# SSM layer of a two-layer hybrid: state updates as four unsplit products on strips of 32 rows, and another split of the PSUM banks

## The chip, the cores and the metric

The kernel runs on one core of a Trainium2 chip. The metric is the device time of one execution, in microseconds. Before the change it is 1091.27 us, the median of three runs (1090.25 to 1092.51).

## The reference, cut to what matters

One inference step of a two-layer encoder for 256 prompt tokens (one sequence) and 128 sample tokens (8 sequences of 16), 384 rows in all, D_MODEL 1024. Layer 0 mixes with short convolutions and attention, layer 1 with a state-space scan (SSM); each layer ends in a convolutional feed-forward network. The change lies in layer 1's mixer:

```python
def odd_mixer(h, conv_state, ssm_state, w_in, conv_w, conv_b, dt_bias, a_log, d_skip, norm_w, w_out):
    proj = h @ w_in
    z, xbc, dt_raw = jnp.split(proj, [D_INNER, D_INNER + CONV_DIM], axis=-1)   # 2048, 3072, 32
    xbc, new_conv = causal_dwconv(xbc, conv_state, conv_w, conv_b)
    xbc = jax.nn.silu(xbc)
    xs, bm, cm = jnp.split(xbc, [D_INNER, D_INNER + SSM_GROUPS * D_STATE], axis=-1)
    dt = jax.nn.softplus(dt_raw + dt_bias)
    y, h_last = ssd_scan(xs, dt, a, bm, cm, ssm_state, chunk)
    y = y + d_skip[:, None] * xs
    y = y * jax.nn.silu(z)
    y = rms_norm(y per group, norm_w)
    return y @ w_out, new_conv, h_last

# in ssd_scan, for 32 heads of 64 in 4 groups, state of 128:
    mix = (C·Bᵀ) * decay * dt                 # within a chunk
    y_intra = mix · x
    w_end = exp(cum[:, :, -1:] - cum) * dt
    states = einsum('bcsgn,bcsgr,bcsgrp->bcgrpn', B, w_end, x)    # what a chunk adds to the state
    h_last = exp(cum[-1]) * h0 + states
    y_inter = einsum('bcqgn,bcgrpn,bcqgr->bcqgrp', C, h_in, exp(cum))
```

For the 128 sample tokens each of the 8 sequences is one chunk of 16 with a state h0 of its own; the new state of each of them is an output (`o_hs`).

## The kernel before, in words

Products of activations with weights ("dense" below) run in fp32r with both operands split into a high and a low part: `three` (L404) issues hi·hi, hi·lo, lo·hi, lines 405 to 407. Weights come in blocks through SP's queue, are split by ACT (`wh`) and DVE (`wl`), and are handed out by `W.take`; three tiles of 1024 columns (`wsp`) hold them. Products inside the scan are fp32 or fp32r without a split of the weights.

PSUM has eight banks of 128 x 512 fp32: four in the pool `mm` (`pmm`: the dense products xbc, z, op) and four in `aux` (`paux`: everything else).

The SSM layer goes through four groups of eight heads. For group g, `channels(g)` makes the dense xbc products of that group, the convolution (`conv4`), C·Bᵀ (`cb`, then CB), B transposed (`bT`), and x transposed (`xT`, then `xt`). `scan(g)` runs over three blocks of 128 tokens: b = 0 and 1 are the prompt, b = 2 is the eight sample sequences, 16 rows each. In each block `sg` and `mix` give `y`; in b = 2, `yi` adds what the old states h0 give, and `hn` is what the block adds to them. The scan is interleaved with dense work: it calls `fill(n)`, which takes a few steps of `beside_scan`: `project_z` of this group, `add_out` of the group before (its output product, `op`, which `residual` adds to X), `channels` of the next group. A scheduler with a cost model then orders every engine's instructions anew; its result, not the order of the code, stands in the program.

The state update of b = 2 is done per sequence: `hn` = Bᵀ (128 rows, all but the sequence's 16 zero) times xw. Both are split into halves: `Bh` and `Bl` (eight masked copies each, made by ACT and POOL from `Bd`, `B2`, `Bl2`), and `xs`, which holds for each half of the rows the high part in its own rows and the low part in the other half's. Two fp32r matmuls (L1104, L1105) of 128 x 128 x 512 make one sequence's `hn` in one aux bank; POOL multiplies h0 with its decay E, DVE adds `hn`, and ACT's queue stores the sum. The h0 tiles are loaded by SP's queue (L1095) into seven rotating buffers (`t512("h0", 7)`). `yi` takes four sequences at once: four matmuls of 32 columns each into the four strips of partitions of one bank (L1098), two rounds (`par` 0 and 1: the even and the odd sequences).

The output product of the groups 0 to 2 (`factor is None`) takes four banks at once and goes over the four weight tiles, each for all four banks; the last group's goes bank by bank, with all four weight tiles taken first.

Of the kernel before, what the change touches and what calls it, by code (L numbers as in the profile page):

```python
# [18 lines left out]
P = 128  # L19
NT = 384  # L20
# [15 lines left out]
for _n, _w in _COLS:  # L36
# [2 lines left out]


_CST = [("ident", 128), ("T", 128), ("Ts", 128), ("U", 128), ("Us", 128), ("Tj", 16),
        ("caus", 128), ("smask", 16), ("bmask", 8), ("bmask4", 4), ("nid8", 8), ("nidS", 128), ("hsel", 32), ("ones", 256)]
CCOL, NCST = {}, 0
for _n, _w in _CST:
    CCOL[_n] = (NCST, _w)
# [3 lines left out]
def _constants():  # L49
    c = np.zeros((P, NCST), np.float32)  # L50
    i = np.arange(P)
    k, q = i[:, None], i[None, :]
    same = (k // LB) == (q // LB)

    def put(name, a):
        o, w = CCOL[name]
        c[: a.shape[0], o:o + w] = a

    put("ident", np.eye(P))
    put("T", k <= q)  # L60
# [7 lines left out]
    put("bmask4", ((i % 64) // LB)[:, None] == np.arange(4)[None, :])  # L68
# [166 lines left out]
def build(nc, tc, d, stop=None):  # L235
# [7 lines left out]
    mm = ctx.enter_context(tc.tile_pool(name="mm", bufs=4, space=PSUM))  # L243
    aux = ctx.enter_context(tc.tile_pool(name="aux", bufs=4, space=PSUM))

    def pmm(name):
        return mm.tile([P, 512], F32, tag="mm", name=name)

    def paux(name):
        return aux.tile([P, 512], F32, tag="aux", name=name)  # L250


    X = cp.tile([P, KT, NT], F32, name="X")
# [30 lines left out]
    def act(out, a, f, **kw):  # L284
        S.activation(out, a, f, **kw)  # L285
# [223 lines left out]
        return t[:, 0:w + 256], t[:, w + 256:w + 256 + NB * (LB + w)].rearrange("p (b t) -> p b t", t=LB + w)  # L509

    def finish():
        ctx.close()


# [383 lines left out]


    od = ExitStack()  # L900
    o0 = od.enter_context(tc.tile_pool(name="o0", bufs=1))
    o1 = od.enter_context(tc.tile_pool(name="o1", bufs=2))
    sts = o0.tile([P, 24, NB, 3], F32, name="sts")
# [79 lines left out]
    def channels(g):  # L983

        Bg, Cg = t512("B", 1, (P, NT)), t512("C", 2, (P, NT))
        yield from conv4(16 + g, Bg)
        yield from conv4(20 + g, Cg)
        ps = paux("cb")
        for b in range(3):
            o = slice(b * P, (b + 1) * P)  # L990
            T.matmul(ps[:, o], lhsT=Bg[:, o], rhs=Cg[:, o], start=True, stop=True)
        CB = t512("CB", 2, (P, 3, P))
        tt(CB[:, 0:2, :], ps[:, 0:256].rearrange("p (b q) -> p b q", q=P),
           C("T").unsqueeze(1).broadcast_to([P, 2, P]), ALU.mult)
        tt(CB[:, 2, :], ps[:, 256:384], C("Ts"), ALU.mult)
        ps = paux("bT")
        for b in range(3):
            T.transpose(ps[:, b * P:(b + 1) * P], Bg[:, b * P:(b + 1) * P], ident)
        Bt = t512("Bt", 2, (P, 2, P))
        act(Bt, ps[:, :256].rearrange("p (b n) -> p b n", n=P), AF.Copy)  # L1000

        pB = ps[:, 256:384]
        Bd = t512("Bd", 1, (P, 2, P))
# [24 lines left out]
        return Cg, Cm, CB, Bt, Bh, Bl, xt  # L1028

    def bc64(ap):  # L1030
        return ap.unsqueeze(2).broadcast_to([P, 8, 64])

    def scan(fill, after, g, Cg, Cm, CB, Bt, Bh, Bl, xt):
        h8 = slice(8 * g, 8 * g + 8)

        def col(t, b, off=0):
# [3 lines left out]
        for b in range(3):  # L1040
# [15 lines left out]
            mix = t512("mix", 1, (P, 8, P))  # L1056
# [31 lines left out]
            if b == 2:  # L1088

                pi = paux("yi")  # L1090
                for par in range(2):
                    four = []
                    for i in range(4):
                        h0 = t512("h0", 7)
                        nc.sync.dma_start(out=h0, in_=d["h0"][2 * i + par, g])  # L1095
                        four.append(h0)
                    for i in range(4):
                        T.matmul(pi[32 * i:32 * i + 32, :], lhsT=Cm[:, 2 * i + par, :], rhs=four[i],  # L1098
                                 start=par == 0, stop=par == 1)
                    fill(4)  # L1100
                    for i in range(4):
                        bb, h0 = 2 * i + par, four[i]
                        ph = paux("hn")
                        T.matmul(ph, lhsT=Bh[:, bb, :], rhs=xs[:, bb // 4, :], start=True, stop=False)  # L1104
# [5 lines left out]
                        nc.scalar.dma_start(out=d["o_hs"][bb, g], in_=h0)  # L1110
# [82 lines left out]

    def add_out(yh, yl, factor):
        for m0 in (0, 4):
            if factor is None:
                ps = [pmm("op") for _ in range(4)]
                for kt in range(4):
                    wh, wl = W.take(512)
                    for m in range(4):  # L1200
                        o = slice(m * P, (m + 1) * P)
                        three(ps[m][:, :NT], wh[:, o], wl[:, o], yh[kt], yl[kt], kt == 0, kt == 3)
                        yield
                for m in range(4):
                    residual(m0 + m, ps[m])
            else:
                ws = [W.take(512) for _ in range(4)]
                for m in range(4):
                    ps = pmm("op")
                    for kt in range(4):  # L1210
                        wh, wl = ws[kt]
                        o = slice(m * P, (m + 1) * P)
                        three(ps[:, :NT], wh[:, o], wl[:, o], yh[kt], yl[kt], kt == 0, kt == 3)
                        yield
# [26 lines left out]
    run(add_out(*out))  # L1241
    r = norm_factor(o1)
    od.close()
    if stop == "odd":
        return finish()

# [18 lines left out]
```

## Time and profile before

| | |
|---|---|
| median of three runs | 1091.27 us (1090.25 to 1092.51) |
| the profiled execution | 1090.9 us on the device, span 1089.1 us, granted clock 0.995 |
| busy: PE, DVE, ACT, POOL | 1062.8, 760.8, 502.8, 161.8 us |
| SSM layer | about 457 to 812 us of the span |

PE is TensorE's matmuls, PEld its weight loads, which run beside them. A row of groups reads: line, engine, operation, tile written from tiles read, shape, count, then busy time and the mean duration in ns. A row of waits reads: who waited, for what, then total, times and longest in us. An fp32 matmul leaves two records (two passes), an fp32r matmul one.

### The profile page before, as it was taken

Reading aid. Unit: us, or ns where it says so; the run is one execution under the profiler, and the core shown is the slowest. Engines: PE = TensorE matmul, PEld = TensorE weight load, DVE = VectorE, ACT = ScalarE, POOL = GpSimd, SP = SyncE. Lnnn points to the kernel's source line nnn. Section 1 sums busy time; section 2 is a strip of 40 time slices with the busy share of each in tenths; the row PEclk is TensorE's granted clock in tenths of the full one; section 3 lists DMA queues with packets and bytes.
Section 4 is the critical chain, followed back from the end, with each engine's and each line's share of the span. In section 5 each row is a group of like instructions: output and inputs, shape, how many; then the busy total and the mean of one; then the engine's idle time right before and its main releaser. Section 6 shows DMA issues by size and latency. Waiting matters only on the chain. (4 is left out here: it accounts for less than half of the span.)

```text
span 1089.1 us, 16735 instructions
## 1 busy us (share of the span) xinstructions
PE 1062.8 (98%) x6332; PEld 976.8 (90%) x6332; DVE 760.8 (70%) x1333; ACT 502.8 (46%) x799; POOL 161.8 (15%) x381
## 2 busy tenths in 40 slices
PE   8999999999999999998999999999999999999998
PEld 6788899999999999986876886786799999999998
DVE  6968667777776634487898797798997767775332
ACT  6344334544444433357657275265454444444221
POOL 0030000100000000033261332333302000100000
PEclk9999999999999999999999999999999999999999
DMA  7452534444444443432453444443533434434441
GB/s 275 156 166 62 170 120 129 131 119 133 121 131 126 133 132 121 135 108 88 146 164 123 158 136 137 145 136 129 183 117 124 136 123 129 130 122 143 138 150 42
DMA packets 47945, 146.08 MB, mean 134 GB/s; under 512 B 5720, under 2 KB 7976, under 8 KB 47864
## 3 DMA queue, kind: packets, MB, share of 16 engines
q1 hardware_dynamic: 41976, 132.55, 39.2%
q10 hardware_dynamic: 4608, 8.39, 2.0%
q0 software_dynamic: 1280, 4.06, 1.0%
q8 instruction: 50, 0.82, 0.3%
q14 instruction: 31, 0.25, 0.1%
HBM read 131.61 MB, written 13.37 MB: 133 GB/s over the span
## 5 line engine op out<-in xcount | busy, mean ns | idle before, releaser
L279 DVE TENSOR_TENSOR wl<-raw,wh 128x1024 fp32r<-128x1024 f32 (+1 forms) x205 | 254.9, 1244 | 138.0 <-ACT wh L285 137.1
L285 ACT ACTIVATE wh<-raw 128x1024 fp32r<-128x1024 f32 (+1 forms) x205 | 216.3, 1056 | 241.4 <-PE fd L406 95.0
L405 PE MATMUL fg<-Hh,wh 128*128 128x384 f32 x352 | 118.7, 337 | 0.0
L406 PE MATMUL fg<-Hl,wh 128*128 128x384 f32 x352 | 118.6, 337 | 0.0
L407 PE MATMUL fa<-Hh,wl 128*128 128x384 f32 x352 | 118.4, 336 | 0.0
L406 PE MATMUL fa<-Hl,wh 128*128 128x384 f32 x352 | 118.3, 336 | 0.0
L407 PE MATMUL fg<-Hh,wl 128*128 128x384 f32 x352 | 118.3, 336 | 0.0
L405 PE MATMUL fa<-Hh,wh 128*128 128x384 f32 x352 | 118.3, 336 | 0.0
L405 PE MATMUL fd<-hh,wh 128*128 128x384 f32 x352 | 118.3, 336 | 0.0
L407 PE MATMUL fd<-hh,wl 128*128 128x384 f32 x352 | 118.3, 336 | 0.0
L406 PE MATMUL fd<-hl,wh 128*128 128x384 f32 x352 | 118.3, 336 | 0.0
L282 DVE SCALAR_TENSOR_TENSOR c<-pad,prm,c 128x400 f32<-128x400 f32 (+1 forms) x160 | 107.1, 672 | 7.9 <-ACT c L285 6.1
L406 PEld LDWEIGHTS fg<-Hl,wh 128*128 128x128 f32 x352 | 66.2, 188 | 0.3
L405 PE MATMUL xbc<-Hh,wh 128*128 128x384 f32 x192 | 66.3, 346 | 0.0
L405 PEld LDWEIGHTS fg<-Hh,wh 128*128 128x128 f32 x352 | 66.2, 188 | 0.1
L407 PEld LDWEIGHTS fg<-Hh,wl 128*128 128x128 f32 x352 | 66.2, 188 | 0.1
L406 PEld LDWEIGHTS fa<-Hl,wh 128*128 128x128 f32 x352 | 66.2, 188 | 0.0
L407 PEld LDWEIGHTS fa<-Hh,wl 128*128 128x128 f32 x352 | 66.2, 188 | 0.0
L406 PEld LDWEIGHTS fd<-hl,wh 128*128 128x128 f32 x352 | 66.2, 188 | 0.0
L407 PEld LDWEIGHTS fd<-hh,wl 128*128 128x128 f32 x352 | 66.2, 188 | 0.0
L405 PEld LDWEIGHTS fd<-hh,wh 128*128 128x128 f32 x352 | 66.2, 188 | 0.0
L405 PEld LDWEIGHTS fa<-Hh,wh 128*128 128x128 f32 x352 | 66.2, 188 | 0.0
(825 smaller groups left out, 2206.6 us busy)
## 6 DMA issues: line engine op xcount, KB each, us to landing
raw<-w SPq DMA_DIRECT2D x219, 512.0 KB, 3.5
kc<-kc SPq DMA_DIRECT2D x8, 256.0 KB, 3.9
vc<-vc SPq DMA_DIRECT2D x8, 256.0 KB, 3.0
X<-x SPq DMA_DIRECT2D x8, 192.0 KB, 4.6
o_y<-X SPq DMA_DIRECT2D x8, 192.0 KB, 2.3
o_v<-vt POOLq DMA_DIRECT2D x3, 256.0 KB, 2.6
o_k<-kraw POOLq DMA_DIRECT2D x3, 256.0 KB, 3.3
cst<-cst SPq DMA_DIRECT2D x1, 618.0 KB, 5.7
```

The lines of the kernel that those rows point to most:

```text
L279: (eng or V).tensor_tensor(out=out, in0=a, in1=b, op=op)
L282: V.scalar_tensor_tensor(out=out, in0=a, scalar=s, in1=b, op0=op0, op1=op1)
L285: S.activation(out, a, f, **kw)
L405: T.matmul(out, lhsT=ah, rhs=bh, start=start, stop=False)
L406: T.matmul(out, lhsT=ah, rhs=bl, start=False, stop=False)
L407: T.matmul(out, lhsT=al, rhs=bh, start=False, stop=stop)
```

## The change

- The update of the state uses unsplit fp32 operands. `Bm` holds two masked copies of Bᵀ (`pmask`: the even sequences' rows, the odd ones'), made by two ACT operations. `Bd`, `Bh`, `B2`, `Bl2`, `Bl` and `xs` go.
- Sequences 2i + par, i = 0 to 3, lie in the strip of rows 32i to 32i + 31; masked by parity, a strip of `Bm` and of `xw` holds one sequence. So each round issues four matmuls on strips of 32 rows, one after another into four aux banks, then the four updates of h0. The fill is called four times before them, four times behind them, and four times behind the updates.
- In the SSM layer the banks are divided three (`mm`) to five (`aux`); before and after it four to four.
- `add_out` goes bank by bank in every group.

```diff
+    def share(n, name):
+        if psum:
+            psum["stack"].close()
+        st = psum["stack"] = ExitStack()
+        psum["mm"] = st.enter_context(tc.tile_pool(name="mm" + name, bufs=n, space=PSUM))
+        psum["aux"] = st.enter_context(tc.tile_pool(name="aux" + name, bufs=8 - n, space=PSUM))
...
     od = ExitStack()
+    share(3, "1")
...
-        pB = ps[:, 256:384]
-        Bd = t512("Bd", 1, (P, 2, P))
-        for side in range(2):
-            for half in range(2):
-                act(Bd[64 * half:64 * half + 64, side, :], pB[64 * side:64 * side + 64, :], AF.Copy)
-        Bh = o1.tile([P, NB, P], F32R, tag="Bh", name="Bh", bufs=1)
-        for bb in range(NB):
-            act(Bh[:, bb, :], Bd[:, bb // 4, :], AF.Copy, scale=C("bmask4")[:, bb % 4:bb % 4 + 1])
-        B2 = o1.tile([P, P], F32R, tag="B2", name="B2", bufs=1)
-        act(B2, pB, AF.Copy)
-        Bl2 = t512("Bl2", 1, (P, P))
-        tt(Bl2, pB, f32(B2[:, :]), ALU.subtract)
-        Bl = o1.tile([P, NB, P], F32R, tag="Bl", name="Bl", bufs=1)
-        tt(Bl, Bl2.unsqueeze(1).broadcast_to([P, NB, P]), C("bmask").unsqueeze(2).broadcast_to([P, NB, P]), ALU.mult, G)
+        Bm = t512("Bm", 2, (P, 2, P))
+        for par in range(2):
+            act(Bm[:, par, :], ps[:, 256:384], AF.Copy, scale=C("pmask")[:, par:par + 1])
...
-            if b == 2:
-
-                xs = o1.tile([P, 2, 512], F32R, tag="xs", name="xs", bufs=1)
-                for side in range(2):
-                    own, other = slice(64 * side, 64 * side + 64), slice(64 - 64 * side, 128 - 64 * side)
-                    act(xs[own, side, :], xw[own, :], AF.Copy)
-                    tt(xs[other, side, :], xw[own, :], f32(xs[own, side, :]), ALU.subtract)
...
                     fill(4)
+
+                    ph = [paux("hn") for _ in range(4)]
+                    for i in range(4):
+                        rows = slice(32 * i, 32 * i + 32)
+                        T.matmul(ph[i], lhsT=Bm[rows, par, :], rhs=xw[rows, :], start=True, stop=True)
+                    fill(4)
                     for i in range(4):
                         bb, h0 = 2 * i + par, four[i]
-                        ph = paux("hn")
-                        T.matmul(ph, lhsT=Bh[:, bb, :], rhs=xs[:, bb // 4, :], start=True, stop=False)
-                        T.matmul(ph, lhsT=Bl[:, bb, :], rhs=xs[:, bb // 4, :], start=False, stop=True)
-                        fill(2)
                         tt(heads(h0[:, :]), heads(h0[:, :]), bc64(E[:, 256 + 32 * bb + 8 * g:264 + 32 * bb + 8 * g]),
                            ALU.mult, G)
-                        tt(h0, h0, ph, ALU.add)
+                        tt(h0, h0, ph[i], ALU.add)
                         nc.scalar.dma_start(out=d["o_hs"][bb, g], in_=h0)
+                    fill(4)
...
         for m0 in (0, 4):
-            if factor is None:
-                ps = [pmm("op") for _ in range(4)]
+            ws = [W.take(512) for _ in range(4)]
+            for m in range(4):
+                ps = pmm("op")
                 for kt in range(4):
-                    wh, wl = W.take(512)
-                    for m in range(4):
-                        o = slice(m * P, (m + 1) * P)
-                        three(ps[m][:, :NT], wh[:, o], wl[:, o], yh[kt], yl[kt], kt == 0, kt == 3)
-                        yield
-                for m in range(4):
-                    residual(m0 + m, ps[m])
...
+                if factor is None:
+                    residual(m0 + m, ps)
+                else:
...
     od.close()
+    share(4, "2")
```

In the changed program `three` is at lines 414 to 416, `yi` at 1091, `hn` at 1098, `y` at 1073.

What the scheduler makes of it, at three places on TensorE's queue. First the second group, first round (a row names the line, the tile written and the tiles read, with their numbers). Before, a `yi` strip stands apart from its three fellows:

```order
L1098 MATMUL yi_5987<-h0__5988,Cm1_4531 32x512
L405 MATMUL op_5952<-yh2_4951,wh_5883 128x384
L406 MATMUL op_5952<-yl2_4952,wh_5883 128x384
L407 MATMUL op_5952<-yh2_4951,wl_5884 128x384
L405 MATMUL op_5953<-yh2_4951,wh_5883 128x384
L406 MATMUL op_5953<-yl2_4952,wh_5883 128x384
L407 MATMUL op_5953<-yh2_4951,wl_5884 128x384
L1098 MATMUL yi_5987<-h0__5990,Cm1_4531 32x512
L1098 MATMUL yi_5987<-h0__5992,Cm1_4531 32x512
L1098 MATMUL yi_5987<-h0__5994,Cm1_4531 32x512
```

and after, the four stand together:

```order
L414 MATMUL op_5938<-yh2_4942,wh_5805 128x384
L415 MATMUL op_5938<-yl2_4943,wh_5805 128x384
L416 MATMUL op_5938<-yh2_4942,wl_5806 128x384
L1091 MATMUL yi_5948<-h0__5949,Cm1_4539 32x512
L1091 MATMUL yi_5948<-h0__5951,Cm1_4539 32x512
L1091 MATMUL yi_5948<-h0__5953,Cm1_4539 32x512
L1091 MATMUL yi_5948<-h0__5955,Cm1_4539 32x512
```

Three such tears stood in the old order, none in the new one. Second, the updates and the second round's `yi` in the last group. Before, one update at a time, and the second round's first three strips behind the fourth update (the fourth strip comes 15 `op` products and one update later):

```order
L1104 MATMUL hn_7596<-xs_7497,Bh_7032 128x512
L1105 MATMUL hn_7596<-xs_7497,Bl_7045 128x512
L405 MATMUL op_7603<-yh2_6493,wh_7554 128x384
L406 MATMUL op_7603<-yl2_6494,wh_7554 128x384
L407 MATMUL op_7603<-yh2_6493,wl_7555 128x384
L1098 MATMUL yi_7539<-h0__7621,Cm1_4531 32x512
L1098 MATMUL yi_7539<-h0__7623,Cm1_4531 32x512
L1098 MATMUL yi_7539<-h0__7625,Cm1_4531 32x512
```

After, the first round's four updates stand together, then twelve z products, of which the last three are shown, then the second round's four strips and one of its updates:

```order
L414 MATMUL z2_7258<-wh_7378,Hh_77 128x512
L415 MATMUL z2_7258<-wl_7379,Hh_77 128x512
L416 MATMUL z2_7258<-wh_7378,Hl_78 128x512
L1091 MATMUL yi_7435<-h0__7518,Cm1_4539 32x512
L1091 MATMUL yi_7435<-h0__7520,Cm1_4539 32x512
L1091 MATMUL yi_7435<-h0__7522,Cm1_4539 32x512
L1091 MATMUL yi_7435<-h0__7524,Cm1_4539 32x512
L1098 MATMUL hn_7539<-xw__7396,Bm__6954 128x512
L414 MATMUL op_7514<-yh2_6424,wh_7450 128x384
```

The fourth strip, h0 7524, moved from behind `op` products to its fellows; its tile takes the buffer of the first round's first, 7436. Third, `y` of the second block in the first group (without numbers where a tile has only one). Before it stands in one piece:

```order
L407 MATMUL xbc<-Hh,wl 128x384
L405 MATMUL xbc<-Hh,wh 128x384
L1080 MATMUL y<-xdt__5064,mix__5070 64x64 x16
L1086 MATMUL yi<-S__5062,C__4619 128x512
L1117 MATMUL S<-xw__5066,Bt__4721 128x512
```

and after, the z products, which stood ahead of the scan, are dealt out between its pieces:

```order
L1073 MATMUL y<-xdt__5055,mix__5061 64x64 x2
L414 MATMUL z_4956<-wh,Hh 128x512
L415 MATMUL z_4956<-wl,Hh 128x512
L416 MATMUL z_4956<-wh,Hl 128x512
L1073 MATMUL y<-xdt__5055,mix__5061 64x64 x2
L414 MATMUL z_4957<-wh,Hh 128x512
L415 MATMUL z_4957<-wl,Hh 128x512
L416 MATMUL z_4957<-wh,Hl 128x512
L1073 MATMUL y<-xdt__5055,mix__5061 64x64 x6
L1079 MATMUL yi<-S__5053,C__4627 128x512
```

The `y` products are 192 in both programs; contiguous blocks of them are 40 before and 48 after.

More of the change, by code (lines that the diff above doesn't have):

```diff
@@ L41 @@
 _CST = [("ident", 128), ("T", 128), ("Ts", 128), ("U", 128), ("Us", 128), ("Tj", 16),
-        ("caus", 128), ("smask", 16), ("bmask", 8), ("bmask4", 4), ("nid8", 8), ("nidS", 128), ("hsel", 32), ("ones", 256)]
+        ("caus", 128), ("smask", 16), ("bmask", 8), ("pmask", 2), ("nid8", 8), ("nidS", 128), ("hsel", 32), ("ones", 256)]
 CCOL, NCST = {}, 0
@@ L67, in _constants @@
     put("bmask", (i // LB)[:, None] == np.arange(NB)[None, :])
-    put("bmask4", ((i % 64) // LB)[:, None] == np.arange(4)[None, :])
+    put("pmask", ((i // LB) % 2)[:, None] == np.arange(2)[None, :])
     j8 = np.arange(8)
@@ L242, in build @@
     tiny = ctx.enter_context(tc.tile_pool(name="tiny", bufs=2))
-    mm = ctx.enter_context(tc.tile_pool(name="mm", bufs=4, space=PSUM))
-    aux = ctx.enter_context(tc.tile_pool(name="aux", bufs=4, space=PSUM))
+    psum = {}
+    def share(n, name):
[4 more added lines that the diff above has]
+        psum["aux"] = st.enter_context(tc.tile_pool(name="aux" + name, bufs=8 - n, space=PSUM))
+    share(4, "0")
     def pmm(name):
-        return mm.tile([P, 512], F32, tag="mm", name=name)
+        return psum["mm"].tile([P, 512], F32, tag="mm", name=name)
     def paux(name):
-        return aux.tile([P, 512], F32, tag="aux", name=name)
+        return psum["aux"].tile([P, 512], F32, tag="aux", name=name)
     X = cp.tile([P, KT, NT], F32, name="X")
@@ L511, in finish @@
     def finish():
+        psum["stack"].close()
         ctx.close()
@@ L1027, in channels, with scan @@
             act(xt[:, :, i * P:(i + 1) * P], ps[:, :NT].rearrange("p (b n) -> p b n", n=P), AF.Copy)
-        return Cg, Cm, CB, Bt, Bh, Bl, xt
+        return Cg, Cm, CB, Bt, Bm, xt
     def bc64(ap):
         return ap.unsqueeze(2).broadcast_to([P, 8, 64])
-    def scan(fill, after, g, Cg, Cm, CB, Bt, Bh, Bl, xt):
+    def scan(fill, after, g, Cg, Cm, CB, Bt, Bm, xt):
         h8 = slice(8 * g, 8 * g + 8)
@@ L1195, in add_out @@
         for m0 in (0, 4):
-            if factor is None:
-                ps = [pmm("op") for _ in range(4)]
+            ws = [W.take(512) for _ in range(4)]
+            for m in range(4):
+                ps = pmm("op")
                 for kt in range(4):
-                    wh, wl = W.take(512)
-                    for m in range(4):
-                        o = slice(m * P, (m + 1) * P)
-                        three(ps[m][:, :NT], wh[:, o], wl[:, o], yh[kt], yl[kt], kt == 0, kt == 3)
-                        yield
-                for m in range(4):
-                    residual(m0 + m, ps[m])
[L1206 to L1214, printed above, removed]
+                    wh, wl = ws[kt]
+                    o = slice(m * P, (m + 1) * P)
+                    three(ps[:, :NT], wh[:, o], wl[:, o], yh[kt], yl[kt], kt == 0, kt == 3)
+                    yield
+                if factor is None:
+                    residual(m0 + m, ps)
+                else:
                     o = t512("y", 4, (P, NT))
```

## The prediction

> **What bounds the kernel now.** I read the page first: the busy times, then the chain that ended last. After that the busy times of the SSM layer alone (457 to 812 us, the only stage that the diff touches), what TensorE waited for there, and the timeline around the steps that change. The page:
>
> ```profile
> span 1089.1 us, 16735 instructions
> PE 1062.8 (98%) x6332; PEld 976.8 (90%) x6332; DVE 760.8 (70%) x1333; ACT 502.8 (46%) x799; POOL 161.8 (15%) x381
> PE 29%; DVE 0%; issue 0%
> ```
>
> and the SSM layer (length; then for PE, PEld, DVE, ACT, POOL busy time and count; granted clock; DMA share; GB/s):
>
> ```profile
> 457.00:812.00 355.00, 338.01 (x2007) 278.49 (x2006) 295.77 (x507) 199.74 (x365) 113.06 (x170) 0.99 0.42 136
> ```
>
> TensorE is the bound, in the layer too: 338 of 355 us. So time is won in two ways only: TensorE's stream gets shorter, or the 17 us in which it stands idle shrink. Work that leaves ACT, DVE or POOL counts only where TensorE waits for it. Who it waits for in the layer (total, times, longest):
>
> ```profile
> PE y L1080 <- DVE mix__4959 L279: 2.6, 1, 2.6
> PE y L1080 <- DVE mix__6501 L279: 2.5, 1, 2.5
> PE y L1080 <- DVE mix__7342 L279: 2.5, 1, 2.5
> PE hn L1104 <- DVE y__7502 L279: 1.8, 1, 1.8
> PE yT L587 <- ACT y__4957 L285: 1.6, 1, 1.6
> PE cb L991 <- ACT C__6893 L285: 1.6, 1, 1.6
> PE op L405 <- DVE X L279: 1.1, 1, 1.1
> PE hn L1104 <- DVE xs L279: 0.4, 1, 0.4
> ```
>
> The first three, 7.6 us, are the start of a head group, where ACT and DVE make `mix` from `sg`. The diff leaves that chain as it is, and the new order has as many dense products beside it: no term.
>
> **The state updates (hn).** The timeline around the first group's (start, duration):
>
> ```profile
> 542.76 0.62 PE L1098 MATMUL yi<-h__5330,Cm 128*32 128x512 f32 x1
> 542.78 0.62 PE L1098 MATMUL yi<-h__5336,Cm 128*32 128x512 f32 x1
> ...
> 543.75 0.50 PE L1104 MATMUL hn<-xs,Bh 128*128 128x512 f32 x1
> ...
> 544.32 0.34 PE L405 MATMUL xbc<-Hh,wh 128*128 128x384 f32 x1
> 544.50 0.34 PE L406 MATMUL xbc<-Hl,wh 128*128 128x384 f32 x1
> ...
> 547.14 0.39 PE L1104 MATMUL hn<-xs,Bh 128*128 128x512 f32 x1
> 547.60 0.34 PE L407 MATMUL xbc<-Hh,wl 128*128 128x384 f32 x1
> ```
>
> Durations overlap in the pipeline, so I count from start to start. A pair Bh, Bl costs 547.60 − 547.14 = 0.46 us; behind the four yi it is 544.32 − 543.75 = 0.57. A dense matmul of 384 columns costs 0.17 to 0.18 (544.50 − 544.32). 32 pairs are 14.7 us, with four of them behind yi 15.1.
>
> The new four has no row. It is four fp32 products of 32 rows with 512 columns in four row strips. The nearest row is the four yi: fp32, 512 columns, four column strips; they start within 0.02 us, and the next instruction follows at 543.75, 0.99 after the first. That row strips overlap too is shown for two of 64 rows in the even layer (two matmuls of two passes each):
>
> ```profile
> 90.81 0.70 PE L728 MATMUL s<-KTt,QT 64*128 64x256 f32 x4
> 91.44 0.77 PE L754 MATMUL po<-pts,vt 128*64 128x128 f32 x10
> ```
>
> They took 0.63 us. An fp32 product of 512 columns on the whole array takes, by
>
> ```profile
> 592.82 1.02 PE L1086 MATMUL yi<-S__5764,C__5136 128*128 128x512 f32 x2
> 593.27 0.74 PE L405 MATMUL op<-yh,wh 128*128 128x384 f32 x1
> 593.85 0.34 PE L406 MATMUL op<-yl,wh 128*128 128x384 f32 x1
> ```
>
> 593.85 − 592.82 less one dense 0.17, 0.86 us; so two of 256 columns in turn would take 0.86 and not 0.63. A four lies between 0.99 (overlapped as yi) and 4 x 0.86 = 3.44 (in turn). I take 0.99, the row of the same type, length and number of strips.
>
> Around a block of another shape the dense stream loses a little on both sides. One small block, `y` of four records:
>
> ```profile
> 532.76 0.33 PE L407 MATMUL xbc<-Hh,wl 128*128 128x384 f32 x1
> 533.02 0.34 PE L1080 MATMUL y<-xdt__5186,mix__5197 128*64 128x64 f32 x4
> 533.28 0.44 PE L405 MATMUL xbc<-Hh,wh 128*128 128x384 f32 x1
> 533.56 0.34 PE L406 MATMUL xbc<-Hl,wh 128*128 128x384 f32 x1
> ```
>
> 532.76 to 533.02 is 0.26 where 0.17 is usual, 533.28 to 533.56 is 0.28: 0.20 for the two sides. So a four between dense products costs 1.2 us. In the new order six of eight fours stand together, two (first and last group) are torn into one and three. One piece alone is this row, 553.23 − 552.26 = 0.97, with its sides 1.17:
>
> ```profile
> 552.26 1.05 PE L1098 MATMUL yi<-h__5477,Cm 128*32 128x512 f32 x2 [0.34 <-DMA h__5477<-h]
> 553.23 0.44 PE L406 MATMUL xbc<-Hl,wh 128*128 128x384 f32 x1
> ```
>
> 6 x 1.2 + 4 x 1.17 = 11.9, against 15.1: **−3.2 us**. The Trainium skill, "TensorE: Matmul & The Clock Gate", Part 3 (Measured speedup vs the span model), gives 3.07 times for four row strips of 32 with N=512; on 3.44 that would be an estimate of 1.12 for a four, and −2.2 for this term. The trace, for column strips of that length, has 3.44/0.99 = 3.5.
>
> **yi** keeps its matmuls. In the old order three of its eight fours are torn (one strip apart from three), in the new one none, since the fill is dealt out elsewhere. Each tear is one piece of 1.17: **−3.5**.
>
> **y.** The new order has 48 blocks of `y` among the dense products where the old had 40: the same 192 matmuls, more often interrupted, above all in the first group, where z now stands between them. The block above takes 0.80 − 2 x 0.17 = 0.45 for four records, mostly its sides (0.20); I take 0.33, the middle, for an additional block: **+2.6** (bounds +1.6 and +3.6).
>
> **ACT, DVE and POOL.** Per group 13 small ACT operations become two, xs goes (two on ACT, two on DVE) and Bl (one on POOL). ACT is busy 200 of 355 us, POOL 113: TensorE's work covers them, and they count nothing by themselves. Three waits stand right behind them. The two of hn, 2.2 us, are in the last group, where DVE is long at xs, slowed by POOL beside it:
>
> ```profile
> 762.16 4.47 DVE L279 TENSOR_TENSOR xs<-xw__7495,xs 64x512 fp32r<-64x512 f32 x2
> 767.27 0.68 DVE L279 TENSOR_TENSOR h__7540<-h__7540,hn 128x512 f32<-128x512 f32 x1
> 767.98 0.34 ACTq L1110 DMA_DIRECT2D o_hs<-h__7540  x1
> 770.04 0.33 SPq L1095 DMA_DIRECT2D h__7627<-h  x1
> 774.11 1.05 PE L1098 MATMUL yi<-h__7627,Cm 128*32 128x512 f32 x2
> ```
>
> With xs gone so are they: −2.2. Of cb and yT, 1.6 each behind ACT, a lighter ACT queue takes a third: −1. Together **−3.2**.
>
> **The output product and the banks.** op <- X, 1.1, is a half that needs four banks while `residual` has not read the last four. Bank by bank it needs one: **−1.1**. The price is that all four weights of a half must be there first; the last group's output product has that form already, and no wait on weights stands among the rows. z takes all three dense banks, so the next product waits for its first Silu; in the first group six z products, y and yi lie between: at least 6 x 0.17 + 0.86 = 1.9 us of cover for one ACT operation; nothing.
>
> **New waits.** pi and four hn fill all five other banks, and the strips are given back by POOL and DVE one after another. In the second and third group more than 30 dense products (5 us) stand behind a four before the next user of a bank; nothing. In the first, the four stands right behind bT and yi and wants the banks of cb and bT, and xT right behind it wants the first hn bank, after one POOL product and one DVE sum:
>
> ```profile
> L279 POOL TENSOR_TENSOR h__5990<-h__5990,E 128x512 f32<-128x512 f32 x1 | 1.0, 1045 | 1.2 <-PE yi L1098 1.2
> ```
>
> 1.0 + 0.7 from the end of yi, less the four's 1.0, and about 0.8 for the banks: +1.5.
>
> The other is the fourth h0 of the second parity. It is loaded into the place of the first parity's first, after sum and store: in the last rows above from the sum's end (767.95) to the yi that uses the load, 6.2 us. Before, that strip stood 15 dense products and an update behind the others and did not wait. Now it stands with its four, and TensorE's queue behind it. In the first group xT and 28 dense products stand between, 28 x 0.17 = 4.8, and the sum is done about as xT starts: 6.2 − 4.8 less a little for xT, +1.0. In the last group, twelve z products between four and yi. With xs gone the sum is done some 0.7 us after the four, the load 6.2 later; a z product takes
>
> ```profile
> 764.86 0.39 PE L405 MATMUL z<-wh,Hh 128*128 128x512 f32 x1
> 765.09 0.40 PE L406 MATMUL z<-wl,Hh 128*128 128x512 f32 x1
> ```
>
> 0.23, twelve 2.8: a wait of 4.1, or 2.7 if store and load come 1.4 sooner; +3.4. New waits together **+5.9** (bounds +2 and +9).
>
> **The clock.** In two stretches, each right after a wait on mix, TensorE ran at half clock:
>
> ```profile
> 513.20:520.10 6.90, 6.32 (x42) 4.98 (x43) 5.36 (x7) 2.77 (x5) 1.96 (x1) 0.51 0.44 123
> 748.70:752.10 3.40, 3.40 (x21) 1.90 (x20) 1.84 (x4) 2.09 (x5) 1.04 (x1) 0.50 0.58 186
> ```
>
> At full clock they take half: up to 5.1 us could be won; the new long wait could add one, 1.7 lost. The wait on mix__6501 was as long and had none, so it hangs on little. I take 0.
>
> **Sum**: −3.2 − 3.5 + 2.6 − 3.2 − 1.1 + 5.9 = −2.5. The profiled execution took 1090.9 us on the device (span 1089.1, 1.8 around it), 0.4 below the median of the three runs, 1091.27. By the one 1088.4, by the other 1088.8; I say 1088.5.
>
> **The rivals.**
> - *The fours run in turn* (slower). Nothing in the trace shows four row strips at once; in turn a four costs 3.44 + 0.2 = 3.6, eight 29 us against 15.1: +13.9 instead of −3.2, 1088.5 + 17.1 = 1105.6. It decides, the other terms being +0.7, from 14.4/8 = 1.8 us a four on. Against it speak the strips at 90.81. Chance 0.08.
> - *The banks and the reloads take more* (slower). At the upper bound of the new waits, +9, and two half-clock stretches behind them, +3.4: 1088.5 + 6.5 = 1095. For it: all five banks are held at once. The Trainium skill, "TensorEngine Tiling (Array Packing)", Gotcha 1 (PSUM Pressure) and PSUM Bottleneck, says that row tiles write to different banks and that emptying them may become the bound; by that rule this case comes true. Against it: POOL is idle two thirds of the layer. Chance 0.15.
> - *More than I count* (faster). The reloads come sooner (+2 instead of +5.9) and the half-clock stretches at the start of groups go (−3): 1088.5 − 6.9 = 1081.6. Chance 0.23.
>
> **The numbers.** My forecast has 0.46; its own range, by the bounds of y and half those of the waits, is 1085.5 to 1091.5. 0.2%, 2.2 us, is about what a measurement of this kernel can tell from no change; 1089.1 and 1093.5 are the edges. Faster: 0.23, 0.6 of 0.46, and 0.04 of the 0.08 left over: 0.55. Slower: 0.23 less 0.02 of the second rival: 0.21. Within: 0.24. The range 1080 to 1096 leaves out the fours in turn and the outer parts of the other two.
>
> **What would show it.** In the profile after: four hn records that start within 0.05 us of each other and give way after about 1 us (right), or 0.86 apart (first rival). No torn yi. A wait of yi on a DMA of h0 in the last group, 2.7 to 4.1 us, in the first about 1. The waits op <- X and hn <- xs gone. TensorE busy in the layer near 334 us, its idle time about 18. Half-clock stretches: two as now, none, or three. I would be wrong above all if a four took 2 us or the reloads did not wait.

## The result, and the profile after

The changed kernel takes 1119.77 us (median of 4 runs, 1115.95 to 1122.07) against 1091.89 us before (1090.25 to 1093.37): a ratio of 1.0252, 95% interval 1.0217 to 1.0288. It is 27.9 us slower, where 2.8 us faster was forecast. The profiled execution is the shortest of the four (1115.95). Its page, the same lines that the prediction shows of before:

```profile
span 1114.1 us, 16682 instructions
PE 1070.3 (96%) x6332; PEld 973.6 (87%) x6332; DVE 751.0 (67%) x1321; ACT 481.2 (43%) x743; POOL 148.6 (13%) x377
PE 25%; DVE 0%; ACT 0%; issue 0%
```

DVE, ACT and POOL do less, as intended, and TensorE is busy 7.5 us longer and idle 17.5 us longer. To see where, I cut both traces at three marks: the first `xbc` product, the last `op` product of the SSM layer, and the last `fa` product of the feed-forward network that follows. Before they lie at 457.4, 808.9 and 989.5, after at 458.3, 819.5 and 1014.5. So the layer takes 9.7 us more and the piece behind it 14.4; what lies outside these two adds 0.9.

**The piece behind the layer** is the larger one, and the prediction does not speak of it. TensorE's timeline (start, duration) at the layer's end, before:

```profile
808.93 0.34 PE L407 MATMUL op<-y2tdr,wl 128*128 128x384 f32 x1
809.11 0.34 PE L405 MATMUL fa<-Hh,wh 128*128 128x384 f32 x1
...
817.00 0.72 PE L484 MATMUL ss<-cst,acc 128*128 128x1 f32 x6
...
823.02 0.91 PE L498 MATMUL Rp<-D,cst 128*128 128x384 f32 x2
```

and after; in brackets stands how long TensorE stood idle, and for whom:

```profile
819.51 0.34 PE L416 MATMUL op<-y2tdr,wl 128*128 128x384 f32 x1
827.33 1.44 PE L493 MATMUL ss<-cst,acc 128*128 128x1 f32 x6 [7.48 <-DVE acc L288]
831.91 1.65 PE L507 MATMUL Rp<-D,cst 128*128 128x384 f32 x2 [3.14 <-DVE D L505]
834.13 0.69 PE L414 MATMUL fa<-Hh,wh 128*128 128x384 f32 x1 [0.58 <-ACT R L294]
...
837.18 0.46 PE L414 MATMUL fa<-Hh,wh 128*128 128x384 f32 x1
837.47 0.34 PE L415 MATMUL fa<-Hl,wh 128*128 128x384 f32 x1
```

Before, the feed-forward network's `fa` products begin 0.18 us behind the last `op`, and the norm's two small steps (`ss`, then `Rp`) are dropped into that stream when DVE has made their operands: the list of TensorE's waits of before is empty from there on. After, `fa` comes 14.62 us behind the last `op`, because the diff writes `share(4, "2")` behind `norm_factor`. The new banks are carved out of those that the norm's own tiles hold, so `fa` must wait until `Rp` has been read (`R`, on ACT), and the norm's chain of DVE steps, 7.48 + 3.14 + 0.58 us of idle time, lies bare. DVE was late in any case, with two weight splits ahead of the last sums:

```profile
819.75 2.36 DVE L288 TENSOR_TENSOR wl<-raw,wh 128x1024 fp32r<-128x1024 f32 x2
...
823.49 0.55 DVE L288 TENSOR_TENSOR y__7954<-op,zs__7684 128x384 f32<-128x384 f32 x1
```

On top of that, TensorE runs at half clock from 824 us on, in the gap and for 3.4 us of dense products behind it (third column from the right):

```profile
824.00:837.50 13.50, 6.45 (x19) 5.23 (x20) 5.69 (x22) 2.44 (x5) 1.07 (x5) 0.50 0.13 49
```

**Inside the layer**, from its first `xbc` to its last `op`, before and after (length; busy times of PE, PEld, DVE, ACT, POOL):

```profile
457.40:809.10 351.70, 334.71 (x1988) 275.19 (x1987) 292.87 (x503) 197.73 (x362) 113.06 (x170) 0.99 0.43 137
```

```profile
458.20:819.70 361.50, 338.42 (x1986) 269.77 (x1986) 280.60 (x490) 174.81 (x306) 103.16 (x166) 0.97 0.40 132
```

TensorE's idle time went from 17.0 to 23.1 us and its busy time from 334.7 to 338.4. The granted clock, summed over windows of 1 us, gives 10.2 us at half clock before and 20.5 after; if half of such time is lost, that is 5.1 us, more than the whole growth of the busy time. The waits of after in the layer:

```profile
PE cb L1002 <- ACT C__6005 L294: 3.6, 1, 3.6
PE cb L1002 <- ACT C__6818 L294: 3.0, 1, 3.0
PE y L1073 <- DVE mix__6432 L288: 2.9, 2, 2.1
PE y L1073 <- DVE mix__7243 L288: 2.9, 2, 2.1
PE yi L1091 <- DMA h__7524<-h: 2.8, 1, 2.8
PE y L1073 <- DVE mix__4950 L288: 2.5, 1, 2.5
PE xT L1026 <- ACT sq__5278 L294: 1.2, 1, 1.2
PE xT L1026 <- ACT sq__5479 L294: 0.9, 1, 0.9
PE yT L597 <- DVE y__7313 L288: 0.8, 1, 0.8
PE yi L1091 <- DMA h__5442<-h: 0.6, 1, 0.6
```

`op <- X`, `hn <- y` and `hn <- xs` are gone. In their place `cb` waits 6.6 us where it waited 2.6, and `yi` waits for the reload of `h0`. Why `cb` is late, DVE's timeline shows in the second group; first before, then after:

```profile
625.79 0.61 DVE L279 TENSOR_TENSOR pad<-xbc,R 128x256 f32<-128x256 f32 x2
626.32 0.67 DVE L279 TENSOR_TENSOR h__6097<-h__6097,hn 128x512 f32<-128x512 f32 x1
```

```profile
627.81 0.68 DVE L288 TENSOR_TENSOR h__6049<-h__6049,hn 128x512 f32<-128x512 f32 x1
...
630.27 0.68 DVE L288 TENSOR_TENSOR h__6055<-h__6055,hn 128x512 f32<-128x512 f32 x1
...
631.35 0.61 DVE L288 TENSOR_TENSOR pad<-xbc,R 128x256 f32<-128x256 f32 x2
```

`pad` opens the convolution whose result is C; `cb` needs C. Before, one update's sum stood near it, behind it. Now four sums stand ahead of it, with one `y` product among them, and `pad` starts 5.6 us later in the trace. The sums are some 2.4 us of this (4 x 0.6), and 0.8 is the later start of the layer; the rest is other work that also stands ahead of `pad` or takes longer there.

### The profile page after: what moved, and what is told of

Its sections match the earlier page's. It is cut to its first block, busy times and chain, and to the rows that moved or that the text cites. A ratio compares the mean times of both kernels' runs of the same rounds, so it can differ in the third digit from the quotient of the medians.

```text
span 1114.1 us, 16682 instructions
## 1 busy us (share of the span) xinstructions
PE 1070.3 (96%) x6332; PEld 973.6 (87%) x6332; DVE 751.0 (67%) x1321; ACT 481.2 (43%) x743; POOL 148.6 (13%) x377
## 5 line engine op out<-in xcount | busy, mean ns | idle before, releaser
L288 DVE TENSOR_TENSOR wl<-raw,wh 128x1024 fp32r<-128x1024 f32 (+1 forms) x205 | 251.5, 1229 | 129.5 <-ACT wh L294 129.1
```

The lines of the kernel that those rows point to most:

```text
L288: (eng or V).tensor_tensor(out=out, in0=a, in1=b, op=op)
```

## The experiments

Each is compared with runs of the kernel before on the same chip, 1091.94, 1091.87 and 1091.49 us in the three groups of runs. I give the time and the ratio to before with its interval.

**e8, the new banks by themselves.** To the kernel before, only the opening of new pools is added, at both ends of the layer and with the old sizes:

```diff
     od = ExitStack()
+    share(4, "1")
...
     od.close()
+    share(4, "2")
```

> The kernel before with its PSUM pools closed and opened again at the two ends of the SSM layer, four and four each time; nothing else. Theory: a new pool's first product waits for the last reader of the old pool's bank: at the start of the layer 0.7 us, at its end the 4.3 us that the early return showed, and 3.4 to 6.8 us at half clock behind it: 6 to 9 us more, 1098 to 1101. Rival: with no change of size nothing moves: 1091 to 1093.

1100.87 us, 1.0080 (1.0065 to 1.0095): 9.0 us for a change that moves no arithmetic and no sizes. In the list of waits and in TensorE's timeline, the first products behind the layer:

```profile
PE fa L413 <- DVE y__8074 L287: 4.3, 1, 4.3
PE xbc L413 <- DVE X L287: 0.7, 1, 0.7
```

```profile
816.45 0.66 PE L413 MATMUL fa<-Hh,wh 128*128 128x384 f32 x1 [4.34 <-DVE y__8074 L287]
816.91 0.52 PE L414 MATMUL fa<-Hl,wh 128*128 128x384 f32 x1
```

The old pools would have given `fa` a bank that had long been read; the new one gives it the bank of the last `op`. Dense products that start 0.17 us apart at full clock start 0.32 apart here, until 824.5.

**e1, the hand-over ahead of the norm.** The changed kernel with one line moved, so that `ss` and `Rp` are no longer ahead of `fa`:

```diff
     run(add_out(*out))
+    share(4, "2")
     r = norm_factor(o1)
     od.close()
-    share(4, "2")
```

> The changed kernel with the return to four and four banks placed ahead of norm_factor (the last norm's ss and Rp) and not behind it; on TensorE's queue only ss and Rp change places with the first fa products. Theory: the four dense banks of the last division reach over a bank of the five that ss and Rp still held, so ffn1's first product could not start before Rp; that is 14.4 us from the last op to the first fa less about 1 for ss and Rp, and 1.6 at half clock behind it: 15 us less than the changed kernel's 1119.8, about 1105, and no idle time ahead of ss. Rival: fa had to wait for the norm's inputs anyway (acc, Hl, weights): then the order alone changes nothing, 1117 to 1121.

1113.27 us, 1.0188 (1.0157 to 1.0220): 6.5 us less than the changed kernel, not the 15 expected. The waits of `ss` and `Rp` are gone, and in the list of waits stands the one of e8:

```profile
PE fa L414 <- DVE y__7954 L288: 4.3, 1, 4.3
```

Moving the line saves the norm's chain but not the wait for the last bank, nor the half clock behind it. I had put the whole gap down to the norm.

**e10, no hand-over behind the layer.** The changed kernel without the last `share(4, "2")`; three and five banks stay to the end of the program:

```diff
     od.close()
-    share(4, "2")
```

> The changed kernel with one thing undone: the banks are not shared out anew behind the SSM layer, 3 and 5 stay to the end; h0 keeps its 7 buffers. If the hand-over behind the layer costs about 15 us (idle 7.5 + 3.1 + 0.6 before and in the norm, and half clock behind it): 1105 to 1107, and the two fours of e5_no_switch_back (1104.9) differ from it by the reloads alone, 2 to 4 us, so 1107 to 1109. If instead those 15 us only move to the next place where DVE is behind (three banks for fa and fg): 1112 or more.

1108.09 us, 1.0152 (1.0137 to 1.0167): 11.7 us less than the changed kernel. TensorE's order is the same as in the changed kernel up to the last `op` of the layer, row by row. From there to the last `fa` it takes 182.6 us against 194.9, and before 180.6: 2.0 us remain, for three dense banks where the feed-forward network had four. This piece hardly varies: it takes 182.6 us in the traces of all four kernels that keep three banks to the end (e5, e6, e9, e10), and 180.5 to 180.9 in the three that have four and no hand-over (before, e3, e7). The layer itself shows how much one order can vary: 365.9 us here, 361.5 in the changed kernel's trace,

```profile
460.00:825.90 365.90, 342.40 (x1985) 272.25 (x1986) 280.55 (x490) 174.18 (x306) 101.75 (x166) 0.96 0.41 131
```

with 30.7 us at half clock against 20.5, half of whose difference is 5.1, and 23.5 us idle against 23.1.

**e2, the reload.** The early hand-over of e1, and 11 buffers for `h0` instead of 7, so that the second round's loads need not wait for the first round's stores:

```diff
-                        h0 = t512("h0", 7)
+                        h0 = t512("h0", 11)
```

> The kernel with the early return to four and four banks, and eleven h0 buffers for seven, so that no load of an h0 waits for a store; the order on TensorE is the same. Theory: the waits of yi on the loads (2.8 and 0.6 us) go, with the half-clock stretch behind the longer one (3.4 us, 1.7 lost): 5 us less than the kernel with the early return alone, about 1100. Rival: the loads collide with other transfers, or another wait takes their place (hn on the banks): at most 1 us less.

1109.45 us, 1.0148 (1.0116 to 1.0180): 3.8 us less than with 7 buffers, where 5 were expected; the runs of the two kernels overlap (up to 1112.21 here, from 1110.37 there). The waits of `yi` on a DMA are gone; `yT <- y__7313` rose from 0.8 to 2.4 us, since the last group now runs into DVE instead. The same step without the hand-over behind the layer is e5 against e10: 1104.9 against 1108.09, 3.2 us.

**e5, neither the hand-over behind the layer nor the reload.** The changed kernel with two edits:

```diff
-                        h0 = t512("h0", 7)
+                        h0 = t512("h0", 11)
...
     od.close()
-    share(4, "2")
```

> The changed kernel with eleven h0 buffers and without the return to four and four banks: the three and five stay to the end. Seen in the early return: its first fa waited 4.3 us on DVE's reading of the last op, since the new pool's first bank was one that this op held. Theory: without any return fa takes the oldest of the three banks, which is free, so the last layer's end costs as before the change: the 4.3 us and the half-clock stretch behind them (up to 7 us, 3.4 lost) go, 6 to 8 us less than the early return with eleven buffers (1109.5), about 1102. Rival: three banks are too few for ffn1 (fa, fg, and the next fa while DVE reads): a wait at each of its 22 steps, 1108 or more.

1104.9 us, 1.0108 (1.0086 to 1.0131): 4.6 us less than e2, where 6 to 8 were expected. The long wait of `fa` is gone, and `fg` waits 0.8 us once, not at each step as the rival had it. Most of what is left sits in the layer, where `cb` waits most:

```profile
PE cb L1002 <- ACT C__6005 L294: 3.6, 1, 3.6
PE cb L1002 <- ACT C__6818 L294: 3.6, 1, 3.6
```

**e4, the sums left out.** On e2's kernel DVE's four sums of the second round are left out in the second and third group. If the bunched sums made `cb` late, its waits should go.

```diff
-                        tt(h0, h0, ph[i], ALU.add)
+                        if not (g in (1, 2) and par):
+                            tt(h0, h0, ph[i], ALU.add)
```

> Early return, eleven h0 buffers, and in the second round of the groups 2 and 3 of 4 (g = 1 and 2) DVE's sum h0 + hn is left out (the stored state is h0 times its decay there). Theory: cb waits 3.6 and 3.0 us because four sums stand together on DVE ahead of the convolution that makes C; without the eight sums the cb waits fall to about 1 us each and the half-clock stretches behind them go (2 x 1.7): 8 us less than with the sums, about 1092. Rival: C is late for another reason (ACT's table loads and weight splits): the waits stay within 0.7 us and the time within 2 us of the kernel with the sums.

1114.02 us, 1.0184 (1.0147 to 1.0222), which is not faster, and `cb` waits 4.6 us twice instead of 3.6. The scheduler filled the room with the chain of the group's norm, which waits for ACT first and stands ahead of `pad`:

```profile
631.04 0.17 DVE L1179 TENSOR_SCALAR v<-ssq 128x3 f32<-128x3 f32 x1 [0.79 <-ACT xdt__6230 L294]
...
633.23 0.16 DVE L291 SCALAR_TENSOR_TENSOR rg<-rqb,rqo 128x3 f32<-128x3 f32 x1
633.30 0.61 DVE L288 TENSOR_TENSOR pad<-xbc,R 128x256 f32<-128x256 f32 x2
```

Both forecasts missed: the waits grew by 1.0 us, and the time by 4.6. So this run neither confirms nor refutes the sums: `pad` is late either way, behind other work. What it shows is that less work on DVE is not enough while something else stands ahead of `pad`.

**e6, the same work dealt out differently.** The kernel of e5 (1104.9), with 6, 2 and 4 dense products behind `yi`, `hn` and the sums instead of 4, 4 and 4:

```diff
                                  start=par == 0, stop=par == 1)
-                    fill(4)
+                    fill(6)
...
                         T.matmul(ph[i], lhsT=Bm[rows, par, :], rhs=xw[rows, :], start=True, stop=True)
-                    fill(4)
+                    fill(2)
```

In the second and third group the second four then stands behind `cb`, and C's convolution ahead of the four sums.

> The same (no return, eleven buffers), and the twelve fills of a round dealt out as 6 ahead of the four updates, 2 behind them, 4 behind the sums (before 4, 4, 4). In the planned order of the groups 2 and 3 the second four then stands behind cb, and on DVE the convolution that makes C ahead of the sums. Theory: C is late because the four sums stand ahead of its convolution on DVE (the run without sums did not tell, since the norm's chain took their place there): the cb waits of 3.6 us each fall to about 1 and their half-clock stretches go, 5 to 8 us less than the run without the return. Rival: the delay moves to the next user of DVE (xT, yT or y): within 2 us of it.

1099.24 us, 1.0066 (1.0050 to 1.0082): 5.7 us less, as expected. First the layer without the new fill, then with it, then TensorE's new order around `cb`:

```profile
457.40:820.40 363.00, 340.52 (x1986) 273.26 (x1987) 281.49 (x490) 174.47 (x306) 103.46 (x166) 0.95 0.39 132
```

```profile
459.20:815.80 356.60, 333.54 (x1986) 267.00 (x1987) 280.48 (x490) 174.81 (x306) 106.36 (x166) 0.98 0.40 134
```

```profile
616.27 1.14 PE L1098 MATMUL hn<-xw__5868,Bm__5272 32*128 32x512 f32 x8
...
634.70 0.94 PE L1002 MATMUL cb<-C__6005,B__6004 128*128 128x128 f32 x6 [1.47 <-ACT C__6005 L294]
...
635.89 2.18 PE L1098 MATMUL hn<-xw__5868,Bm__5272 32*128 32x512 f32 x8
```

`cb` waits 1.5 us twice instead of 3.6 twice, but the layer's idle time is not less: 22.5 us, then 23.1, because `xT`, `op` and `mix` take what `cb` gives. The gain is all in the busy time, 340.5 to 333.5, and with it go the half-clock times, 34.2 to 13.7 us. It is not a chance of one trace: the granted clock of the whole execution is 0.984 to 0.988 in the four runs of e5 and 0.990 to 0.994 in those of e6. So the gain came through the clock. Part of it is given back: the second four, right behind `cb` and `bT`, now lasts 2.18 us, the first 1.14.

**e3, the output product alone.** The kernel before with only the part of the diff in `add_out`: four weights taken first, one bank at a time instead of four.

```diff
-                ps = [pmm("op") for _ in range(4)]
+            ws = [W.take(512) for _ in range(4)]
+            for m in range(4):
+                ps = pmm("op")
```

> The kernel before with only the output product taken bank by bank in every group; banks four and four throughout, updates split as before. Prediction's step: the wait of op on X, 1.1 us, goes, and nothing else: about 1090.5. Rival: the other order of the weights or the residuals in the midst of the scan delay DVE's chain: 2 to 5 us more, 1093 to 1096.

1091.06 us, 0.9990 (0.9976 to 1.0003): no change clear of noise, which leaves room for the expected 1.1. In the trace `op <- X` is gone, and the two waits of `cb` are 1.9 + 1.9 where they were 1.6 + 1.0.

**e7, old banks, strips in pairs.** The changed kernel without any hand-over, four and four banks throughout, two unsplit strips at a time, 11 buffers for `h0`:

```diff
-    share(3, "1")
...
-                    ph = [paux("hn") for _ in range(4)]
-                    for i in range(4):
+                    for two in (0, 2):
+                        ph = [paux("hn") for _ in range(2)]
...
-    share(4, "2")
```

> Unsplit updates on strips of 32 rows, but two at a time, with fill(2) behind each pair and behind its sums; four and four banks throughout with no new pools; output product bank by bank; eleven h0 buffers. Theory: what the change lost lies in the division of the banks and in the bunching of the sums, not in the unsplit product: a pair costs about 1.06 + 0.2 us, sixteen are 20 against 15.1 for the 32 split pairs, +5, less 2.2 for the waits behind xs: about 1094. Rival: it lies in the unsplit products (the planner takes them to be longer than they are and sets the other engines' order by that): 1100 or more.

1102.91 us, 1.0098 (1.0075 to 1.0121), against 1094 expected; the rival had 1100 or more. Behind the layer nothing is lost (180.5 us); the layer alone is 11.4 us longer than before. Its busy times, and three rows of TensorE's timeline:

```profile
459.60:822.70 363.10, 342.03 (x1988) 269.35 (x1987) 281.55 (x491) 175.05 (x306) 103.18 (x166) 0.98 0.40 132
```

```profile
543.72 1.19 PE L1098 MATMUL hn<-xw__5171,Bm__4723 32*128 32x512 f32 x4
...
548.15 1.13 PE L1098 MATMUL hn<-xw__5171,Bm__4723 32*128 32x512 f32 x4
549.20 0.45 PE L414 MATMUL xbc<-Hh,wh 128*128 128x384 f32 x1
```

A pair takes 1.05 us (549.20 − 548.15), as long as a four, so 16 pairs cost twice the eight fours. By this row 16 x 1.05 is already 16.8 us, against the 14.7 that the prediction worked out for the 32 old split pairs. Idle time is 21.1 us against 17.0, and half clock 17.1 us against 10.2, of which I estimate half as lost. So unsplit updates can cost 11 us with the old banks too, when they are placed like this; whether the scheduler's order makes it, as the rival says, this run does not tell.

**e9, the banks without the new updates.** The kernel before with the output product bank by bank, and three and five banks from the layer's start to the program's end:

```diff
     od = ExitStack()
+    share(3, "1")
```

> The updates stay split and one at a time, as before; the output product goes bank by bank, and the banks are shared out 3 and 5 from the SSM layer's start to the program's end (one hand-over, none behind the layer). It tells apart what is left of e6_fill_6_2_4 (1099.24, 7.3 above before). Theory A, the seven us belong to the rewritten updates (fours behind which work stands bunched): this kernel is within 2 us of before, 1091 to 1093. Theory B, they belong to three dense banks instead of four and to the one hand-over: 1096 to 1099. By the rows of e5 and e6 the hand-over at the start is 0.7 (xbc behind X) and three banks show as fg behind pad 0.8 and op behind zs 0.9, 2.4 together; I expect 1094.

1096.06 us, 1.0042 (1.0028 to 1.0055): 2 us above what I expected, and at the lower edge of theory B. The layer:

```profile
459.70:812.00 352.30, 333.65 (x1986) 275.83 (x1987) 288.45 (x502) 194.00 (x360) 110.03 (x170) 0.98 0.42 136
```

Within the layer the trace is 0.6 us longer (352.3 against 351.7), less than one order varies there, and the piece behind it 2.0. The rest, 2.4 us, stands ahead of the layer's first `xbc`, of which `xbc <- X` is 0.7; the remainder is spread that I can't assign (the mark lies between 457.4 and 460.0 in traces whose programs are alike up to there). So of the 7.2 us that e6 is above before, 4.6 are there with the old updates too, and 2.6 are left for the new ones. With the two intervals that is barely clear of noise; in the traces the layer of e6 is 4.3 us longer than that of e9.

## Why the prediction was wrong

The runs make a chain from before to the changed kernel: three and five banks +4.6 us (e9); the new updates on top, at the best fill tried, +2.6 (e6 less e9, by the ratios); the diff's own fill +5.7 (e5 less e6); 7 buffers for `h0` +3.2 (e10 less e5); the hand-over behind the layer +11.7 (the changed kernel less e10). That they add up to 27.8 of the 27.9 measured proves nothing, since each step starts where the one before it ends. The sizes are rough: by the ratios the last three are 4.6, 4.8 and 10.9. The hand-over is the surest: the piece behind the layer is 12.3 us longer in the changed kernel's trace than in e10's, and this piece repeated to 0.1 us in four kernels.

- **The step that failed** is the first: "the SSM layer alone (457 to 812 us, the only stage that the diff touches)". `share(4, "2")` acts on the first product behind the layer. Its cost, some 14 us in the trace and 11.7 against a kernel without it, was in no term, no rival and no bound. The diff shows the line, and in the changed kernel it stands behind `norm_factor`, which issues `ss` and `Rp`. The price could have been read from the trace of before: there, `Rp` starts 14.1 us behind the last `op` (823.02 − 808.93), time covered by `fa` and `fg`, the products that the line holds back. e8 and e1 show that moving the line would not have been enough: `fa` then waits 4.3 us for the last `op` to be read.
- **The clock, "I take 0"**, with at most 1.7 us lost. In the layer half-clock time doubled, 10.2 to 20.5 us, an estimated 5 us of loss. In the layer of the changed kernel each wait of 2.1 us or more had such a stretch beside it. The prediction looked for TensorE busy near 334 us there and idle about 18; it was busy 338.4 and idle 23.1. e6 shows that this term can be worth a whole rearrangement.
- **"In the second and third group ... nothing"** of the new waits. That sentence looked at who needs a bank. The price came through DVE's order instead: four sums ahead of `pad`, and `cb` waits 6.6 us instead of 2.6, where the prediction had it wait less. e6 shows that moving the four away takes this wait down; e4, that taking the sums away alone does not.
- **hn and yi**: right on the mechanism. No `yi` is torn, and six fours of `hn` stand together. Four row strips overlap; a four takes 1.07 us, between the row of `yi` (0.99) and the estimate from the Trainium skill, "TensorE: Matmul & The Clock Gate", Part 3 (1.12). In TensorE's timeline of the last group, the four and the product behind it:

```profile
769.15 1.14 PE L1098 MATMUL hn<-xw__7396,Bm__6954 32*128 32x512 f32 x8
770.22 0.50 PE L414 MATMUL z<-wh,Hh 128*128 128x512 f32 x1
```

  The rival of fours in turn is out. The sum of hn, yi and y, −4.1 us of TensorE's stream, can't be confirmed: busy time less half of the half-clock time fell by 1.4, but by 6.2 and 2.6 in e5 and e10, whose orders up to the layer's end are the changed kernel's but for a few swapped `yi` strips.
- **The reload**: right. The last group's `yi` waited 2.75 us where 2.7 to 4.1 was forecast, the first group's 0.6 where it said 1.0, and both together were worth 3.2 to 3.8 us, against +4.4. TensorE's timeline of the last group:

```profile
777.74 1.05 PE L1091 MATMUL yi<-h__7524,Cm 128*32 128x512 f32 x2 [2.75 <-DMA h__7524<-h]
```

- **The banks of the first group**, +1.5: TensorE stood idle 1.2 us ahead of `xT` there, but the list of waits names ACT's `sq` as what came last, so the bank is not shown to be the cause.
- **The output product**, −1.1 alone: gone as a wait; e3 does not show it as time, and in its trace `cb` waits 1.2 us more. The wait seems to have moved on, to the next place where DVE is late.
- **The rival "banks and reloads take more"** had the right resource and the wrong place: it priced the five banks inside the layer at some 6.5 us. The Trainium skill, "TensorEngine Tiling (Array Packing)", Gotcha 1 (PSUM Pressure), which the prediction weighed there, says that different row tiles write to different banks. The four does take four banks here, but emptying them did not become the bound: `hn` does not stand in the list of waits of the changed kernel at all. The measured cost of banks is in handing them over (11.7 us) and in keeping three (2.0 behind the layer).

What stays open: how much of the 2.6 us of the updates would go with yet another fill, why e7 loses 11 us in the layer, and what the 1.7 us ahead of the layer in e9 are. No kernel tried here is faster than the kernel before by more than the noise.

## What to carry to other kernels

A change of how banks are shared has a cost at its borders: list what the first instruction behind the border must now wait for, and what small dependent steps the old stream covered there. If a hand-over is needed, keep it away from a place where a chain of small dependent steps is hidden behind dense work. When instructions are grouped so that one engine does four at once, the engine behind it gets four in a row too, and what is queued behind those on that engine is what comes late.

## What the runs showed of the hardware that I had not expected

- Half clock came in stretches of about 3.4 us or a multiple of it (6.8 behind `cb` in e10, 10.3 behind the layer in e8), most of them beside an idle time of TensorE or up to 3 us behind it. Two of the six in the changed kernel, behind `cb` (3.6 us idle, up to 636.0) and behind `yi` (2.75, up to 777.7), with the granted clock third from the right:

```profile
636.00:639.40 3.40, 3.39 (x14) 3.40 (x15) 3.37 (x10) 1.95 (x6) 2.09 (x4) 0.51 0.38 95
```

```profile
779.10:782.50 3.40, 3.40 (x10) 2.43 (x9) 2.62 (x4) 0.00 (x0) 0.81 (x1) 0.54 0.19 12
```

  All six idle times of 2.1 us or more in that layer had one; before, of the three of 2.5 to 2.6 us two. Of two of 1.92 us in e9 one had, the two of 1.47 us in e6 had none, but a wait of `xT` of 1.55 us in e5 had one (562.9 to 566.3). So these runs give no sharp limit. If half of such time is lost, each stretch of 3.4 us cost up to 1.7 us beyond the wait itself, and that is most of why two executions of one order (the layer in the changed kernel and in e10) differ by 4.4 us.
- Row strips of 32 overlap so fully that two take as long as four: 1.05 us in e7, 1.07 in the changed kernel.
